# New priorities for the list schedule of a hybrid encoder's first phase, with both embedding projections ahead of its last scan

## The chip, the cores and the metric

The kernel runs on one core of one Trainium2 chip. The metric is device time in microseconds (us) of one execution, median over the runs shown. TensorE is called PE below, VectorE DVE, ScalarE ACT, GpSimd POOL, and SyncE SP; SP only issues transfers (DMA).

## The reference, cut to what matters

Two encoder layers over 512 tokens of width 1024, everything in fp32, with a ConvFFN of inner width 2816 and a gated embedding in each layer:

```python
def reference(x, p, ...):
    h = x
    for i in range(2):
        if i == 0:
            z = rmsnorm(h, mix_norm[0]) @ mix_w_in[0]
            y_a = rwkv7_bidir(z[..., :RWKV_COLS], ...)      # 8 heads x 64, one scan in each direction
            y_b = hyena_bidir(z[..., RWKV_COLS:], ...)      # 512 channels, long filters by FFT
            h = h + jnp.concatenate([y_a, y_b], axis=-1) @ mix_w_out[0]
        else:
            z = rmsnorm(h, na_norm[0]) @ na_w_qkv[0]
            h = h + neighbourhood_attention(z, ...) @ na_w_out[0]
        h = h + conv_ffn(h, ffn_norm[i], ffn_w_up[i], ffn_conv_w[i], ffn_conv_b[i], ffn_w_down[i])
        h = h + per_layer_embedding(h, p[i], ple_norm[i], ple_w_gate[i], ple_w_proj[i])
    return h

def per_layer_embedding(h, p_i, norm_g, w_gate, w_proj):
    return jax.nn.sigmoid(rmsnorm(h, norm_g) @ w_gate) * (p_i @ w_proj)
```

The product `p_i @ w_proj` (512x256 by 256x1024) depends on nothing else, so that it can be made at any time before its layer's end.

## The kernel before, in words

Tokens lie along the free axis, channels along the 128 partitions; a tile is 128x512. A product of fp32 operands is made as three matmuls (`mm3`): both operands are split into a high and a low part, ACT makes the high part by a cast and POOL the low part by a subtraction, and high x high, high x low and low x high are summed in PSUM.

Layer 0's mixing is the first phase (`mixer0`, `both_mixers`). The rest (`ffn`, `ple`, `mixer1`, and the same again) follows it, with `gemm` as its main loop; weights come there by `load_split` into `wraw` (128x1024), ACT casts them to `whi` (line L633), DVE makes `wlo` (L625), and PE multiplies them into the bank `g` (L619). In front of a `gemm` stands `norm`: for each of the eight tiles of h, ACT makes the scaled and split input `xh` and the square `nsq` (both L628; two buffers of `nsq`), and POOL adds the squares up one after the other (`nacc`, L625).

The first phase isn't written in the order of execution. An object `Plan` stands in for the compiler's engines: each call becomes one or more steps in a named group, 2741 steps in all; a step knows its engine, the steps it must come after, and a price (`Plan.note`, `price`). `ranks` gives each step the longest path of prices from it to the end, lifts it to at least the rank of its group's first step less `DRAG`, and adds 1000 times the priority of its group, from the tables `ORDER` and `MOVED` (method `order` of `Kern`). A list scheduler (`schedule`) then goes through the engines, takes the ready step of highest rank, and keeps account of free tiles, and `write` issues the steps in that order. `in_order` holds the compiler to it, each engine by itself. Since all steps are issued in `write`, every instruction of this phase has line L582 in the profile, and its names tell what it is.

The groups that matter here:

- `z`, `prep`, `inverse`, `scan`, `out`, each for m = 0 to 3: RWKV for two heads each. `z` is the input projection, `prep` (m, d) prepares direction d, and stores for `inverse` the products of 64x64 blocks that have to be inverted. `inverse` m loads those (tiles `nd`), solves on DVE by a row of small multiplications and reductions that grow from 128x1 to 128x225, stores the solution (`xd`), loads it back transposed (`w<-xd`, eight transfers), and goes on with matmuls `b<-w` 64x64 on PE. `scan` m then runs over eight chunks of 64 tokens, one after the other in a chain: matmuls of 64 columns into a bank (`b<-uv,w`, `b<-uv,dg`, `b<-x,uv`, `b<-r,w`), a copy from PSUM by ACT and DVE into `uv`, matmuls on that copy (`b<-x,uv`), and so on. Between two links of that chain PE can only do what other groups have ready.
- `hyena`, `filters`, `fparts`, `kf`, `signals`, `ab`, `back`: the long convolutions, as matmuls with tables of the Fourier transform (`dft_f`, `dft_i`). `kf` are the four transforms of the filters and `ab` those of the signals, 24 matmuls of 128x512 and less each, `back` the inverse transforms.
- `early`, `mid`, `last`: the output projection (`mix_w_out`) over parts of the channels. The last parts need the end of the last `scan` and of `back`.
- `emb` l: the projection `p @ w_proj` of layer l, 48 matmuls of 128x512. Its weights and inputs come through `wr` (`in_proj`, `in_pT`), its eight results go to DRAM (`pj_d_125` to `pj_d_132` for layer 0, `pj_d_133` to `pj_d_140` for layer 1), and `ple` loads them much later.

Loads of weights and tables go through three buffers `wr` and are issued by SP, which issues all transfers of the phase in one order and waits at the first that can't start. The parts made from them lie in twelve buffers `wp`; other tiles are `w`, of 39.

## Time and profile before

| | |
|---|---|
| median of three runs | 1597.96 us (1595.04 to 1604.57) |
| the profiled execution | 1599.19 us, of which 1597.4 us from the first to the last instruction |
| mean granted clock of PE | 0.976 |
| PE busy | 1527.6 us (96%) |
| DVE, ACT, POOL busy | 975.3 (61%), 718.5 (45%), 341.6 us (21%) |
| last matmul of the first phase | ends at 499.4 us |
| first matmul of the rest | starts at 508.25 us |

The page of a profile gives busy time by engine, then the span in 40 slices, the DMA queues, the chain of work that ended last, the costliest groups of instructions and the DMA issues. Answers of the trace used below are: the table of stretches (start:end, length, then busy us and count of instructions of PE, PE's weight loads, DVE, ACT and POOL, the granted clock of PE as a share of full speed, the busy share of the DMA engines, GB/s); the timeline of one engine (start, length, engine, line, instruction, count, and in brackets the idle time before it with what ended it); and groups by line and shape (count, busy us, mean ns of one, idle time before). A tile's name is shown without its number.

### The profile page before, as it was taken

The numbers are of one execution on the slowest core, as the hardware profiler recorded it, in microseconds if no ns is written. First come the engines' busy times: TensorE is split into PE (matmuls) and PEld (weight loads), VectorE is DVE, ScalarE is ACT, GpSimd is POOL, SyncE is SP. The second block draws the span as 40 slices with busy tenths as digits, with TensorE's granted clock in tenths as the row PEclk, the third lists the DMA queues.
The fourth block names the chain that finished last, engine by engine and source line by source line (L and its number), as shares of the span: only waits on it lengthen the run. The fifth ranks groups of instructions, "written<-read, shape, count | busy, mean of one in ns | idle before, by whom it ended". The sixth has DMA issues, their size and how long they took to land.

```text
span 1597.4 us, 24570 instructions
## 1 busy us (share of the span) xinstructions
PE 1527.6 (96%) x9520; PEld 1217.7 (76%) x9520; DVE 975.3 (61%) x1618; ACT 718.5 (45%) x1210; POOL 341.6 (21%) x296
## 2 busy tenths in 40 slices
PE   7999999979897999999999999999999999999997
PEld 6766777757585888888888878777778888888886
DVE  5875777865644567535675664555666664276654
ACT  5636464644444444313444554555554442244432
POOL 5664464443463000000002231021030000000020
PEclk9998999979898999999999999999999999999999
DMA  7456474777354223222342324223122332322421
GB/s 240 121 133 195 129 213 119 229 204 231 113 183 138 93 92 101 97 93 92 106 145 93 104 98 134 82 93 120 60 72 77 103 106 98 100 92 86 166 93 66
DMA packets 114583, 195.97 MB, mean 123 GB/s; under 512 B 27537, under 2 KB 57105, under 8 KB 114466
## 3 DMA queue, kind: packets, MB, share of 16 engines
q1 hardware_dynamic: 114466, 194.40, 38.5%
q8 instruction: 75, 1.23, 0.3%
q14 instruction: 42, 0.34, 0.1%
HBM read 163.95 MB, written 28.84 MB: 121 GB/s over the span
## 4 chain that ended last, share of the span: by engine, by line
PE 82%; DVE 6%; DMA 4%; ACT 3%; SPq 2%; issue 1%; POOL 1%; POOLq 0%; DVEq 0%; ACTq 0%
PE g L619 61%; PE b L582 17%; DVE w L582 4%; SPq L582 2%; PE m L619 2%; PE s L619 1%; DMA wr<-in_mix_w_in 1%; PE m L1878 1%; POOL w L582 1%; ACT w L582 1%; DMA w<-nd 1%; DMA wr<-in_dft_f 1%; POOL nacc L625 0%; ACT oh L633 0%; DVE uv L582 0%
## 5 line engine op out<-in xcount | busy, mean ns | idle before, releaser
L625 DVE TENSOR_TENSOR wlo<-wraw,whi 128x1024 fp32r<-128x1024 f32 x180 | 227.8, 1267 | 322.5 <-ACT whi L633 317.7
L633 ACT CAST whi<-wraw 128x1024 fp32r<-128x1024 f32 x180 | 188.2, 1046 | 406.7 <-PE g L619 398.5
L619 PE MATMUL g<-xh,whi 128*128 128x512 f32 x832 | 326.8, 393 | 8.9 <-ACT whi L633 8.9
L619 PE MATMUL g<-xh,wlo 128*128 128x512 f32 x832 | 325.3, 391 | 1.0 <-DVE wlo L625 1.0
L619 PE MATMUL g<-xl,whi 128*128 128x512 f32 x832 | 325.0, 391 | 0.0
L619 PEld LDWEIGHTS g<-xh,whi 128*128 128x128 f32 x832 | 157.0, 189 | 43.1 <-ACT whi L633 9.3
L619 PEld LDWEIGHTS g<-xh,wlo 128*128 128x128 f32 x832 | 156.8, 189 | 34.7 <-DVE wlo L625 1.7
L619 PEld LDWEIGHTS g<-xl,whi 128*128 128x128 f32 x832 | 157.1, 189 | 32.4
L625 POOL TENSOR_TENSOR nacc<-nsq 128x512 f32<-128x512 f32 x5 | 8.8, 1769 | 760.3 <-PE g L619 639.7
L582 PE MATMUL b<-xh,wp 128*128 128x512 f32 x432 | 149.9, 420 | 10.3 <-ACT wp L582 10.0
L619 PE MATMUL g<-hh,whi 128*128 128x512 f32 x352 | 137.2, 390 | 0.0
L619 PE MATMUL g<-hh,wlo 128*128 128x512 f32 x352 | 137.0, 389 | 0.0
L619 PE MATMUL g<-hl,whi 128*128 128x512 f32 x352 | 136.9, 389 | 0.0
L622 DVE SCALAR_TENSOR_TENSOR c<-u,prm,c 128x511 f32<-128x511 f32 x176 | 126.3, 746 | 6.4 <-ACT c L628 5.9
L582 PEld LDWEIGHTS b<-xh,wp 128*128 128x128 f32 x432 | 82.3, 195 | 35.1 <-ACT wp L582 12.0
L628 ACT ACTIVATE c<-u,prm 128x512 f32<-128x512 f32 x88 | 70.3, 817 | 70.8 <-DVE u L625 70.8
L582 POOL TENSOR_TENSOR wp<-wr,wp 128x512 fp32r<-128x512 f32 x62 | 83.1, 1352 | 48.2 <-ACT wp L582 41.3
L582 POOL TENSOR_TENSOR w<-w 128x256 f32<-128x256 f32 (+2 forms) x69 | 76.1, 1121 | 69.2 <-ACT w L582 51.8
L582 PE MATMUL b<-xl,wp 128*128 128x512 f32 x216 | 88.6, 416 | 0.0
L625 DVE TENSOR_TENSOR u<-g,rstd 128x512 f32<-128x512 f32 x104 | 71.3, 686 | 16.4 <-PE g L619 15.6
L582 DVE TENSOR_TENSOR w<-w 128x512 f32<-128x512 f32 (+16 forms) x116 | 69.1, 613 | 17.6 <-DMA w<-nd 10.7
L619 PE MATMUL g<-wlo,xh 128*128 128x512 f32 x192 | 77.2, 402 | 0.0
(181 smaller groups left out, 2608.1 us busy)
## 6 DMA issues: line engine op xcount, KB each, us to landing
wraw<-in_up SPq DMA_DIRECT2D x88, 512.0 KB, 3.5
wraw<-in_down SPq DMA_DIRECT2D x44, 512.0 KB, 3.5
wr<-in_mix_w_in SPq DMA_DIRECT2D x52, 256.0 KB, 3.8
wraw<-in_na_w_qkv SPq DMA_DIRECT2D x24, 512.0 KB, 3.5
x<-ch_d SPq DMA_DIRECT2D x16, 640.0 KB, 5.7
ch_d<-w SPq DMA_DIRECT2D x64, 128.0 KB, 2.2
wraw<-in_gate SPq DMA_DIRECT2D x16, 512.0 KB, 3.4
tab<-in_rpb SPq DMA_DIRECT2D x8, 768.0 KB, 4.2
```

The source lines that it names most:

```text
L582: getattr(e, method)(*args, **kw)
L619: return self.nc.tensor.matmul(out, lhsT, rhs, start=start, stop=stop, skip_group_check=not group)
L622: return self.nc.vector.scalar_tensor_tensor(out=out, in0=in0, scalar=scalar, in1=in1, op0=op0, op1=op1)
L625: return (eng or self.nc.vector).tensor_tensor(out=out, in0=in0, in1=in1, op=op)
L628: return self.nc.scalar.activation(out=out, in_=in_, func=func, **kw)
L633: self.nc.scalar.copy(h, src)
L1878: nc.tensor.transpose(pst[:, i], sc[:, i // 2, (i % 2) * P:(i % 2 + 1) * P], ident)
```

## The change

The code of the steps is the same, and the same 2741 steps come out with the same things that each must come after. What changes is the priorities, and through them each engine's order in the first phase; the order of all instructions after it is the same in both kernels. The embeddings `emb` go from 25 to 10 in the table, `kf` from 67 to 48, `ab` from 58 to 44, `signals` from 70 to 62, `mid` from 72 to 60, and `MOVED` gives fourteen groups a priority of their own. `DRAG` goes from 0 to 20, so that the steps of a group may differ in rank by up to 20. The other lines add prices for shapes that don't occur in this phase, a switch that has its old value, and a way to chain groups that isn't used here; line numbers grow by 8 or 9, so that the phase's instructions have line L590 in the changed kernel and those of the rest L627, L633, L641 and L655.

```diff
-    DRAG, SMALL = 0.0, 3
+    DRAG, SMALL = 20.0, 3
...
+        if engine == "tensor" or dma:
+            before = self.final.get((self.behind.get(self.group), engine))
+            if before is not None:
+                s.after[before.n] = True
+            self.final[self.group, engine] = s
...
+                if rows > 64 and n > 64:
+                    t = max(n / 2000, 0.057)
...
-                 hyena=50, fparts=40, kf=67, signals=70, ab=58, back=46, early=30, emb=25, consts=86, mid=72,
-                 last=99)
+                 hyena=50, fparts=40, kf=48, signals=62, ab=44, back=46, early=30, emb=10, consts=76, mid=60,
+                 last=99, norm1=98, next=40)
...
-    MOVED = {("back", 0): 57.5, ("back", 2): 35.5, ("early", 0): 28.5, ("hyena", 2): 26.5, ("kf", 0, 1): 30.5,
-             ("mid", 1): 32.5, ("scan", 0): 86.5, ("early", 1): 36.5}
+    MOVED = {("ab", 0): 84.5, ("ab", 1): 38.5, ("back", 0): 57.5, ("early", 1): 36.5, ("hyena", 2): 26.5,
+             ("inverse", 2): 88.5, ("kf", 0, 1): 30.5, ("kf", 1, 1): 49.5, ("mid", 0): 61.5, ("mid", 1): 32.5,
+             ("out", 3): 60.5, ("prep", 1, 0): 84.5, ("hyena", 0): 59.5, ("hyena", 3): 68.5}
```

Three places show what that makes of the order. The first is PE's queue at the end of scan 2, where no other group stood between the links of the chain before (`b<-w` 64x128 are the last products of `prep`, `b<-con,w` transposes):

```order
L582 MATMUL b<-x,uv 64x64 x4
L582 MATMUL b<-r_637,w 64x64 x4
L582 MATMUL b<-w 64x128 x7
L582 MATMUL b<-uv,x 64x64 x4
L582 MATMUL b<-x,uv 64x64 x4
L582 MATMUL b<-w 64x128 x11
L582 MATMUL b<-uv,w 64x64 x4
L582 MATMUL b<-uv,dg 64x64 x4
L582 MATMUL b<-con,w 128x128 x8
```

In the changed kernel the same chain has matmuls of 128x512 of hyena 2 (`xh`, `xl` with `wp`) between the copy's two ends:

```order
L590 MATMUL b<-uv,x 64x64 x4
L590 MATMUL b<-x,uv 64x64 x4
L590 MATMUL b<-xh_187,wp 128x512
L590 MATMUL b<-xh_190,wp 128x512
L590 MATMUL b<-xl_191,wp 128x512
L590 MATMUL b<-xh_190,wp 128x512
L590 MATMUL b<-xl_191,wp 128x512
L590 MATMUL b<-xh_190,wp 128x512
L590 MATMUL b<-xh_169,wp 128x512
L590 MATMUL b<-xl_170,wp 128x512
L590 MATMUL b<-uv,w 64x64 x4
L590 MATMUL b<-uv,dg 64x64 x4
```

Between links of scan 2 that had nothing between them stand now eight matmuls and more. Counted over the whole queue, 84 matmuls of 128x512 of other groups stand inside scan 2 (48 before), and 128 (44 before) between the last product that inverse 3's store needs and inverse 3's first matmul, among 344 matmuls of all kinds there (252 before). From the like product to inverse 1's first matmul there are 236 (386 before), 76 of them of 128x512 (86 before); for inverse 2 332 (362 before), 72 of 128x512 (82 before); for inverse 0 230 (222 before), 134 of 128x512 (122 before).

The second place is PE's queue where the phase ends and `g` begins. Before, 38 and ten more matmuls of layer 1's embedding (`b<-w,wp`) stand there, among those of the output projection:

```order
L582 MATMUL b<-w,wp 128x512 x38
L582 MATMUL b<-xh_811,wp 128x512
L582 MATMUL b<-xl_812,wp 128x512
L582 MATMUL b<-xh_811,wp 128x512
L582 MATMUL b<-xl_812,wp 128x512
L582 MATMUL b<-xh_811,wp 128x512
L582 MATMUL b<-xl_812,wp 128x512
L582 MATMUL b<-xh_811,wp 128x512 x3
L582 MATMUL b<-w,wp 128x512 x2
L582 MATMUL b<-xh_811,wp 128x512
```

In the changed kernel the phase ends with the output projection alone:

```order
L590 MATMUL b<-xh_811,wp 128x512 x4
L590 MATMUL b<-xh_1143,w 128x512
L590 MATMUL b<-xh_1145,w 128x512
L590 MATMUL b<-xl_1146,w 128x512
L590 MATMUL b<-xh_1145,w 128x512
L590 MATMUL b<-xl_1146,w 128x512
L590 MATMUL b<-xh_1145,w 128x512
L590 MATMUL b<-xl_1146,w 128x512
L590 MATMUL b<-xh_1145,w 128x512
L627 MATMUL g<-xh_6042,whi 128x512
```

Behind the last matmul of scan 3 stand 160 matmuls of 128x512 (212 before) and 84 of 128x256 (96 before). Inside scan 3 there are 96 of other groups' 128x512 in both kernels.

The third place is SP's queue at the same boundary. Before, the stores of layer 1's embedding stand ahead of the first load of the next stage:

```order
L582 DMA wr<-in_mix_w_out_b 128x512 x8
L582 DMA wr<-in_proj 128x512 x3
L582 DMA wr<-in_mix_w_out_b 128x512
L582 DMA wr<-in_proj 128x512
L582 DMA wr<-in_mix_w_out_b 128x512
L582 DMA pj_d_133<-w 128x512
L582 DMA pj_d_134<-w 128x512
L582 DMA pj_d_135<-w 128x512
L582 DMA pj_d_136<-w 128x512
L582 DMA pj_d_137<-w 128x512
L582 DMA pj_d_138<-w 128x512
L582 DMA pj_d_139<-w 128x512
```

In the changed kernel the loads of `wraw` follow the last loads of `wr`:

```order
L590 DMA w<-bon_d_116 128x512
L590 DMA wr<-in_dft_i 128x512 x2
L590 DMA w<-in_xT 128x512
L590 DMA wr<-in_mix_w_out_a 128x512 x3
L590 DMA w<-in_xT 128x512 x3
L590 DMA wr<-in_mix_w_out_b 128x512 x10
L655 DMA wraw<-in_up 128x1024 x24
```

All sixteen stores of `pj_d` have moved ahead of the end of scan 3. One of them, `pj_d_125`, stands now between inverse 3's store of `xd` and its eight loads `w<-xd`; 19 loads into `wr` (eight of `in_proj`, four of `in_pT`, seven of `dft_f`) stand in SP's queue around that place.

9 lines of the change are left out of this document (5 added, 4 removed).

## The prediction

> **What bounds the kernel now.** I read the page's share of engines and its chain of waits first:
>
> ```profile
> PE 1527.6 (96%) x9520; PEld 1217.7 (76%) x9520; DVE 975.3 (61%) x1618; ACT 718.5 (45%) x1210; POOL 341.6 (21%) x296
> PE 82%; DVE 6%; DMA 4%; ACT 3%; SPq 2%; issue 1%; POOL 1%; POOLq 0%; DVEq 0%; ACTq 0%
> PE g L619 61%; PE b L582 17%; DVE w L582 4%; SPq L582 2%; PE m L619 2%; PE s L619 1%; DMA wr<-in_mix_w_in 1%; PE m L1878 1%; POOL w L582 1%; ACT w L582 1%; DMA w<-nd 1%; DMA wr<-in_dft_f 1%; POOL nacc L625 0%; ACT oh L633 0%; DVE uv L582 0%
> ```
>
> PE is busy for 96% of the span and makes 82% of the chain. Both kernels give PE the same matmuls, so only two things can change: the time in which PE waits, and the time in which its clock is at half speed. I call both together the loss. The second view, the table of stretches, shows where it is. The cuts are at places named below: 320.6 is the end of the last product that inverse 3's store needs (p), 360.7 inverse 3's first matmul (q), 378.4 to 433.4 is scan 3, 499.4 the phase's last matmul.
>
> ```profile
> 20.00:320.60 300.60, 287.75 (x3133) 216.34 (x3133) 218.02 (x422) 160.80 (x340) 161.96 (x158) 0.97 0.57 163
> 320.60:360.70 40.10, 29.30 (x255) 22.02 (x255) 27.40 (x66) 17.35 (x41) 17.31 (x16) 0.79 0.72 210
> 360.70:378.40 17.70, 17.33 (x301) 13.58 (x301) 8.63 (x16) 7.91 (x17) 5.66 (x5) 1.00 0.88 284
> 378.40:433.40 55.00, 46.86 (x467) 34.43 (x467) 35.13 (x55) 21.79 (x59) 25.00 (x21) 0.88 0.42 134
> 433.40:499.40 66.00, 63.75 (x320) 51.77 (x318) 31.95 (x48) 27.37 (x48) 29.39 (x24) 1.00 0.44 146
> 499.40:508.20 8.80, 0.00 (x0) 0.00 (x0) 2.52 (x4) 6.52 (x12) 3.97 (x4) 0.69 0.83 298
> 508.20:516.50 8.30, 7.28 (x16) 5.28 (x17) 5.50 (x3) 3.66 (x5) 7.52 (x4) 0.50 0.52 145
> 516.50:1597.00 1080.50, 1064.24 (x5001) 866.10 (x4999) 633.59 (x990) 459.70 (x670) 83.52 (x49) 0.99 0.30 99
> 339.00:356.00 17.00, 11.17 (x71) 8.81 (x72) 14.16 (x33) 6.38 (x15) 6.90 (x5) 0.50 0.74 246
> ```
>
> Per microsecond the loss is largest in four places: p to q (idle 10.8 of 40.1, clock 0.79), scan 3 (idle 8.1, clock 0.88), and the boundary in two rows (8.8 with nothing done, then 8.3 at clock 0.50). The tail after scan 3 loses 2.25 of 66, and all behind 516.5 is the same code in the same order. So the change is worth what it does to p to q, scan 3, the boundary and the long early stretch.
>
> The timeline of PE shows what the idle time from p to q is:
>
> ```profile
> 313.13 0.45 PE L582 MATMUL b<-uv,x 128*64 128x64 f32 x8 [1.62 <-DVE uv L582]
> 319.52 1.08 PE L582 MATMUL b<-w 64*64 64x128 f32 x22
> 337.01 0.45 PE L582 MATMUL b<-uv,w 128*64 128x64 f32 x8 [2.95 <-ACT uv L582]
> 337.39 0.45 PE L582 MATMUL b<-uv,dg 64*64 64x64 f32 x8
> 345.27 1.02 PE L582 MATMUL b<-x,uv 128*64 128x64 f32 x8 [2.56 <-ACT uv L582]
> 348.06 2.93 PE L582 MATMUL b<-w,wp 128*128 128x512 f32 x6 [1.77 <-ACT wp L582]
> 360.67 1.55 PE L582 MATMUL b<-w 64*64 64x64 f32 x42
> ```
>
> PE waits for scan 2's own copies (`uv`) with nothing else to do, while the solve of inverse 3 goes on elsewhere; from 339 on the clock is at half speed too.
>
> **The change, part by part.** *Work and loss from p to q.* At full speed the work is 29.30 less half of the 11.17 done at half speed, 23.7; the loss is 40.1 - 23.7 = 16.4 us. The price of what is moved in comes from groups by line and shape, the first row from 484 to 499.4, the second from 435 to 484:
>
> ```profile
> L582 PE MATMUL b<-w,wp 128*128 128x512 f32 x48 | 11.6, 394 | 0.0
> L582 PE MATMUL b<-w 128*128 128x256 f32 x96 | 12.7, 288 | 0.6 <-POOL w L582 0.6
> ```
>
> The first gives 11.6/48 = 0.242 us each, the second 0.132. There are 128 matmuls of 128x512 from p to q instead of 44: 84 x 0.242 = 20.3 us. Small ones come at 0.38 per eight (337.01 to 337.39), 0.047 each, and the eight other matmuls that are more add 0.4. The work is 44.4 us. The chain behind p (store, loads, DVE's solve, store, loads) took 40.1 in the trace, itself stretched by what else DVE and SP did, so it is covered by work alone with some 4 us over. Where are the 84 from? 36 are hyena 2's, which stood ahead of p, the others are the embeddings' and filter transforms'. No work vanishes, so I count losses only. What loss stays: the last chunk of scan 2 is still bare by the order; I leave it 3 us of waits (2.56 was one before) and 1.5 for a half-speed stretch of 3.4 us. The term is 16.4 - 4.5 = **11.9 us gained**. The bounds: nothing gained, if what is moved in isn't ready (rival 2), and 16.4.
>
> *Scan 2 ahead of p.* The last ten microseconds:
>
> ```profile
> 311.00:321.00 10.00, 7.53 (x150) 6.55 (x148) 9.65 (x19) 4.97 (x14) 4.38 (x4) 0.83 0.42 141
> ```
>
> The idle time is 2.5, and clock 0.83 is 3.4 us at half speed, worth about 1.3. The order puts hyena 2's matmuls into nine links that were bare (the fences on scan 2), eight at a time, 8 x 0.242 = 1.9 us against a wait of 1.62. Of 3.8 lost I take **3 as gained**. Half speed began here although no wait was longer than 1.62. The Trainium skill ("TensorE: Matmul & The Clock Gate", section "Why this matters for your kernels") asks for no idle gaps of PE above about 3 us to keep the clock; by that rule a bare chunk with waits like these would cost no clock at all, and the sum would come out 1.5 us lower. The trace shows otherwise, and I stay with the trace.
>
> *q to scan 3, and scan 3.* The first lost 0.4 and is full still. In scan 3 the order has 96 matmuls of 128x512 of others as before, and as many bare links but one; its loss of 8.1 idle plus the half-speed stretches stays: **0**. It could lose or gain 3 us by where the cover falls.
>
> *The tail.* 52 x 0.242 + 12 x 0.132 = 14.2 us of work leave it, but that is work made elsewhere. The cover that it gave is gone: the last split of a weight was early enough before,
>
> ```profile
> L582 POOL TENSOR_TENSOR wp<-wr,wp x62: 1266/1293/1845, 7.2 to 481.7; 128x512 fp32r<-128x512 f32 x62
> ```
>
> at 481.7 + 1.3 = 483.0, 49.6 us behind scan 3's end, with six pieces of the embedding loaded and split among them. Without these (6 x 1.29 = 7.7 us of POOL) some 42 us; the work left is 66 - 2.25 - 14.2 = 49.6. So the splits end ahead of PE by 7 us: **0**, at most 5 lost.
>
> *The boundary.* ACT, PE and SP there:
>
> ```profile
> 498.30 2.03 ACT L582 COPY w<-b 128x512 f32<-128x512 f32 x4
> 500.20 1.97 ACT L628 ACTIVATE xh<-h,prm 128x512 fp32r<-128x512 f32 x3
> 504.63 1.15 ACT L628 ACTIVATE nsq<-h 128x512 f32<-128x512 f32 x2 [1.43 <-POOL nacc L625]
> 506.63 0.63 ACT L628 ACTIVATE nsq<-h 128x512 f32<-128x512 f32 x1 [0.85 <-POOL nacc L625]
> 507.17 1.03 ACT L633 CAST whi<-wraw 128x1024 fp32r<-128x1024 f32 x1
> 508.25 0.79 PE L619 MATMUL g<-xh,whi 128*128 128x512 f32 x1 [8.87 <-ACT whi L633]
> 493.77 6.93 SPq L582 DMA_DIRECT2D pj_d<-w  x8
> 500.80 25.77 SPq L647 DMA_DIRECT2D wraw<-in_up  x8
> ```
>
> The first `g` waited for the cast `whi`, and two queues held that: SP issued the first `wraw` at 500.80, behind eight stores of the embedding; and ACT came to the cast at 507.17 only, behind four copies of the embedding, `xh`, and squares that waited for POOL's sums (1.43 and 0.85). The change frees SP of the stores and ACT of the copies (2.0 us). The squares still stand ahead of `whi` in ACT's queue. From the last addition to h: 0.7 for it, 0.65 for an `xh`, a square 0.6, one wait near 0.9, a square 0.6, the cast 1.0: about 4.5 us instead of 8.9, **4.4 gained**. The half-speed stretch (7.28 busy at 0.50, a loss of 3.6) gets perhaps 0.6 shorter, together **5**. Bounds: 0, if the sums on POOL set it as before, and 8.8.
>
> *SP.* The store `pj_d_125` now stands ahead of the eight `w<-xd` of inverse 3; it waits for an embedding's matmuls and ACT's copy, and behind it wait those loads and then q. The cover of p to q exceeds the chain by 44.4 + 4.5 - 40.1 = 8.8 us, and a delay below that costs nothing: **0**.
>
> *The early part, 20 to p.* The loss is 12.9 us of idle time, and clock 0.97 is 18 us at half speed, some 9 us: 22, of which 3.8 are counted above. The order shifts nearly everything here. Covers of the inverses' chains, as stretches from the like of p to the like of q for m = 0, 1, 2:
>
> ```profile
> 76.30:118.30 42.00, 38.26 (x222) 28.53 (x223) 32.85 (x73) 15.62 (x25) 25.75 (x27) 0.96 0.51 130
> 168.70:210.80 42.10, 38.77 (x389) 29.00 (x388) 27.84 (x68) 16.11 (x39) 19.31 (x20) 0.96 0.41 106
> 241.80:279.00 37.20, 36.00 (x366) 26.16 (x365) 28.44 (x66) 18.02 (x42) 17.49 (x18) 1.00 0.44 110
> 210.76 1.15 PE L582 MATMUL b<-w 64*64 64x64 f32 x32 [0.89 <-POOL w L582]
> ```
>
> By the counts of the order, m = 0 gets 12 more of 128x512 (+2.9), m = 1 loses 10 of them and 140 small ones (2.4 + 6.6 = 9.0, leaving 29.8), m = 2 loses 10 and 20 (3.4, leaving 32.6). Against that, PE itself waited only 0.89 for inverse 1's chain, so the 42.1 is what PE's queue made of it, not its floor; the floor isn't in the trace. I take **1 lost**, between 15 gained (most of the remaining 18) and the 28 of rival 1.
>
> The sum: -11.9 - 3 - 5 + 1 = -18.9 against the profiled execution's 1599.19: 1580.3. That execution was 1.2 above the median, so against the median 1579; I say **1580**.
>
> **Rivals.** *1, slower: the chains of inverse 1 and 2 come bare.* If they take 42.1 and 37.2 as before, the cover is short by 12.3 and 4.6, against 3.3 and 1.2 lost before: 12.4 us more, and each bare stretch may draw a half-speed one like that of 339 to 356, 17 us, worth up to 8.5. With both, 28.4 more: some **1608**. It decides from 26 us of loss in the early part. For it: the shorter cover is certain; against it: the 0.89 above, and the solve competes with less other work. Chance 0.09.
>
> *2, about the same: the hole is one of buffers.* The matmuls moved into it need 19 loads through three buffers `wr`, and PE's wait at 348.06 was for such a part, not for the scan. SP's row:
>
> ```profile
> 341.20 5.61 SPq L582 DMA_DIRECT2D wr<-in_proj  x2
> ```
>
> That is 2.8 us a load, 53 us for 19, and from p to scan 3 there are 44.4 + 4.5 + 17.7 = 66.6. From 3.5 us a load on, the embedding comes too late and PE waits as before; scan 2 and the boundary still gain: 1599 - 8 = **1591** or a little more. Chance 0.15. The Trainium skill ("Perfetto Trace Analysis", section "Optimization Strategy") reads a repeated gap on the engine that should be saturated as a possible sign of too few buffers; by it the changed order would leave the gap. The waits of 2.95 and 2.56 for `uv` say that most of this gap isn't that.
>
> *3, more: the early part gains as well*, 10 of its 18 us: **1570**. Chance 0.13. *4: the tail misses its cover* by 5 to 8 us: 1587. Chance 0.04.
>
> **Chances and range.** The forecast (1572 to 1588) has 0.59. About 0.5%, 8 us, is what a measurement of this kernel can tell from no change, so faster means below 1590 and slower above 1606. Faster: 0.59 + 0.13 + 0.01 of the tail's case = 0.73. Same: rival 2 and the rest of 4, 0.18. Slower: 0.09. The range 1566 to 1597 takes in most of rivals 2 and 3 and leaves out rival 1 and the far end of rival 3.
>
> **What would show it.** From p to q the clock is above 0.9 and the idle time below 5; scan 3 starts near 377 (378.4 less the 13.9 gained ahead of it, plus 12.8 us of work that stands ahead of it now: 14.2 from the tail less 1.4 that went inside scan 3) and takes 55 to 57 us; the phase's last matmul ends near 485; the first `wraw` is issued before that, and `g` starts some 4.5 us behind it. It is wrong if idle time of more than 5 us stands ahead of inverse 1 or 2, if PE waits for `wp` in front of the embedding's matmuls, or if the first `g` still starts 8 us behind.

## The result, and the profile after

The changed kernel takes 1611.51 us (median of 16 runs, 1603.98 to 1625.72), the kernel before 1601.95 beside it (16 runs, 1593.82 to 1606.17). The ratio is 1.0078 with an interval of 1.0061 to 1.0094: slower by about 0.8%, where 1580 and faster was predicted. The profiled execution took 1610.59 us, of which 1608.8 are the span, 11.4 more than the one before.

The page of the changed kernel, busy shares and the chain of waits:

```profile
PE 1536.1 (95%) x9520; PEld 1221.2 (76%) x9520; DVE 976.2 (61%) x1618; ACT 717.9 (45%) x1208; POOL 342.6 (21%) x296
PE 85%; DMA 4%; DVE 3%; ACT 3%; SPq 2%; issue 1%; POOL 1%; DVEq 0%; ACTq 0%; POOLq 0%
```

The line of engine shares in the second row reads DVE 6% in the kernel before and here 3%: DVE left the chain and PE took its place, which alone would look like an improvement. But PE's busy time rose from 1527.6 to 1536.1 us with the same 9520 matmuls, so more of them ran at half speed. The table of stretches of the changed kernel, cut at the places that answer to those of the prediction (326.2 is p, 386.0 q, 406.4 to 460.1 scan 3, 513.1 the phase's last matmul, 518.2 the first `g`):

```profile
20.00:326.20 306.20, 284.85 (x3083) 210.43 (x3081) 209.30 (x412) 153.10 (x325) 159.15 (x155) 0.94 0.55 155
326.20:386.00 59.80, 50.29 (x344) 37.41 (x344) 41.22 (x80) 27.43 (x58) 29.42 (x24) 0.86 0.63 197
386.00:406.40 20.40, 18.83 (x310) 14.71 (x309) 7.76 (x15) 12.37 (x29) 6.25 (x6) 1.00 1.02 305
406.40:460.10 53.70, 47.03 (x478) 35.30 (x477) 33.88 (x55) 23.93 (x60) 25.65 (x22) 0.90 0.47 156
460.10:513.10 53.00, 51.42 (x258) 42.86 (x256) 24.41 (x38) 19.32 (x33) 19.94 (x16) 0.97 0.45 155
513.10:518.20 5.10, 0.00 (x0) 0.00 (x0) 4.76 (x8) 4.09 (x8) 4.14 (x3) 0.98 0.00 0
285.70:326.20 40.50, 39.71 (x707) 30.43 (x702) 29.45 (x59) 22.61 (x57) 18.49 (x18) 1.00 0.72 209
```

Read against the rows in the prediction: from p to q the idle time is 9.5 us (10.8 before) at clock 0.86, where below 5 and above 0.9 were predicted, so the hole is still there. The last row is the stretch from inverse 2's first matmul to p: 0.8 idle at full speed. The tail is 53.0 long instead of 66, and 5.1 us pass before the first `g` instead of 8.8. And the first row, from which some 2 us were to be gained, went from clock 0.97 to 0.94 and from 12.9 to 21.4 us idle. Its cuts, of the changed kernel:

```profile
0.00:118.80 118.80, 99.14 (x582) 73.69 (x582) 78.38 (x142) 58.84 (x96) 68.88 (x79) 0.93 0.58 169
209.30:285.70 76.40, 71.08 (x903) 53.14 (x904) 56.69 (x113) 37.54 (x86) 41.23 (x41) 0.96 0.59 161
```

and the like places of the kernel before:

```profile
0.00:118.30 118.30, 104.83 (x634) 79.55 (x635) 82.86 (x151) 61.65 (x101) 69.51 (x84) 0.99 0.56 163
210.80:279.00 68.20, 66.55 (x838) 49.57 (x839) 53.66 (x110) 39.90 (x88) 37.87 (x36) 1.00 0.63 175
279.00:320.60 41.60, 38.56 (x700) 30.19 (x702) 35.55 (x62) 27.14 (x69) 18.33 (x17) 0.96 0.72 220
```

Inverse 0's first matmul starts at the same time in both (118.8, 118.3), but with 52 matmuls fewer done and a clock of 0.93 instead of 0.99. A ledger puts that in microseconds. The loss up to a place is its time less the work that PE has done by then, each matmul at the full-speed duration of its like in the profile of before. The last column is what the prediction gave for the same stretch:

| up to | loss before | loss after | change in this stretch | predicted |
|---|---|---|---|---|
| inverse 0's first matmul | 12.5 | 26.1 | +13.6 | |
| inverse 2's first matmul | 29.5 | 49.5 | +6.4, with the row above +20.0 | +1 |
| q | 56.4 | 69.9 | -6.5 | -14.9 |
| the phase's last matmul | 71.7 | 85.4 | +0.2 | 0 |
| the first `g` | 80.5 | 90.5 | -3.7 | -4.4 |
| the end | | | +1.4 | -0.6 |
| sum | | | +11.4 | -18.9 |

So 19 of the 30 us of error lie in the early part and 8 around the hole. In single traces such a ledger scatters: two of the kernels below have the same order up to scan 3 (*Its loads first* and *And the link first*), and yet inverse 1's first matmul comes at 204.4 in one and at 210.7 in the other. So a difference of less than some 6 us between two traces, summed up to a place, shows nothing by itself, and verdicts on time go by several runs.

The timeline of the changed kernel at the hole, PE first, then ACT, DVE and SP:

```profile
345.02 3.78 PE L590 MATMUL b<-w,wp 128*128 128x512 f32 x8 [5.70 <-ACT wp L590]
363.32 11.29 PE L590 MATMUL b<-w,wp 128*128 128x512 f32 x38
386.01 2.08 PE L590 MATMUL b<-w 64*64 64x64 f32 x64
344.35 0.62 ACT L590 CAST wp<-wr 128x512 fp32r<-128x512 f32 x1 [6.64 <-DMA wr<-in_dft_f]
346.57 0.69 DVE L590 TENSOR_TENSOR w<-w 128x512 f32<-128x512 f32 x1 [1.92 <-DMA w<-hw_d]
338.81 0.91 SPq L590 DMA_DIRECT2D wr<-in_dft_f  x2
```

PE's longest wait is 5.70 us in front of matmuls of a filter's transform: their part `wp` waits for ACT's cast, the cast waited 6.64 for a load, and SP issued that load at 338.81 only, behind a row of stores and of `w<-hw_d` (the windowed filters). The same wait stands in the three other traces with this order of loads (*Spread*, *And supply*, *And chain* below), with 6.07, 5.79 and 5.07. The 128 large matmuls were there as counted, but the ones that stood first in PE's queue weren't ready, and scan 2's next link stood behind them; 38 others ran in one piece at 363.32, when scan 2 was over. At q PE itself didn't wait: its queue set q, not the inverse.

The timeline of the changed kernel in the early part:

```profile
61.34 0.50 PE L590 MATMUL b<-xh,wp 128*128 128x512 f32 x1 [2.57 <-ACT wp L590]
76.05 1.12 PE L590 MATMUL b<-con,w 128*128 128x128 f32 x4 [2.12 <-POOL w L590]
75.96 4.27 POOL L590 TENSOR_TENSOR wp<-wr,wp 128x512 fp32r<-128x512 f32 x3
57.58 0.54 SPq L590 DMA_DIRECT2D wr<-in_mix_w_in  x1
81.29 0.54 SPq L590 DMA_DIRECT2D wr<-in_mix_w_in  x1
```

and the stretch inside it in which the clock is at half speed:

```profile
67.40:81.10 13.70, 9.78 (x27) 5.87 (x26) 11.88 (x17) 2.71 (x5) 12.83 (x12) 0.50 0.63 155
```

No wait is above 2.57 us, but from 67.4 to 81.1 PE has 27 matmuls only, 18 of `prep` and from 77.45 on nine of `z`, and runs at half speed, while DVE (11.88 of 13.7) and POOL (12.83) are full. SP issued no load of an input weight from 57.58 to 81.29; POOL's three splits at 75.96 come behind `prep`'s additions. How many of the `z` matmuls (those with `wp`) fall between 60 and 80 shows the difference, before:

```profile
60.00:80.00 20.00, 13.68 (x54) 9.46 (x54) 1.85 (x3) 6.46 (x5) 1.00 0.59 168
```

and after:

```profile
60.00:80.00 20.00, 3.28 (x8) 2.37 (x9) 0.62 (x1) 4.04 (x3) 0.69 0.58 152
```

54 before and 8 after (busy us and count of PE, its weight loads, ACT and POOL). These are the two things that the runs had to explain: the loss that is new in the early part, and the hole that stayed.

### The profile page after: what moved, and what is told of

Same layout as the page of the kernel before. It is cut to its first block, busy times and chain, and to the rows that moved or that the text cites. A ratio compares the mean times of both kernels' runs of the same rounds, so it can differ in the third digit from the quotient of the medians.

```text
span 1608.8 us, 24543 instructions
## 1 busy us (share of the span) xinstructions
PE 1536.1 (95%) x9520; PEld 1221.2 (76%) x9520; DVE 976.2 (61%) x1618; ACT 717.9 (45%) x1208; POOL 342.6 (21%) x296
## 4 chain that ended last, share of the span: by engine, by line
PE 85%; DMA 4%; DVE 3%; ACT 3%; SPq 2%; issue 1%; POOL 1%; DVEq 0%; ACTq 0%; POOLq 0%
PE g L627 61%; PE b L590 20%; DMA wr<-in_mix_w_in 2%; SPq L590 2%; DVE w L590 2%; PE m L627 1%; PE s L627 1%; ACT w L590 1%; DMA w<-kt_d 1%; PE m L1887 1%; POOL nacc L633 0%; ACT oh L641 0%; ACT wp L590 0%; DVE ol L633 0%; DVE uv L590 0%
## 5 line engine op out<-in xcount | busy, mean ns | idle before, releaser
L633 DVE TENSOR_TENSOR wlo<-wraw,whi 128x1024 fp32r<-128x1024 f32 x180 | 228.0, 1269 | 315.3 <-ACT whi L641 306.4
L641 ACT CAST whi<-wraw 128x1024 fp32r<-128x1024 f32 x180 | 188.2, 1046 | 408.3 <-PE g L627 400.2
L627 PE MATMUL g<-xh,whi 128*128 128x512 f32 x832 | 326.9, 393 | 5.1 <-ACT whi L641 5.1
L627 PE MATMUL g<-xh,wlo 128*128 128x512 f32 x832 | 325.0, 391 | 2.3 <-DVE wlo L633 2.3
L627 PE MATMUL g<-xl,whi 128*128 128x512 f32 x832 | 325.1, 391 | 0.0
L627 PEld LDWEIGHTS g<-xh,whi 128*128 128x128 f32 x832 | 157.0, 189 | 39.3 <-ACT whi L641 5.5
L627 PEld LDWEIGHTS g<-xh,wlo 128*128 128x128 f32 x832 | 157.0, 189 | 36.1 <-DVE wlo L633 3.0
L627 PEld LDWEIGHTS g<-xl,whi 128*128 128x128 f32 x832 | 157.1, 189 | 32.2
L633 POOL TENSOR_TENSOR nacc<-nsq 128x512 f32<-128x512 f32 x5 | 8.8, 1768 | 753.3 <-PE g L627 639.6
L590 PE MATMUL b<-xh,wp 128*128 128x512 f32 x432 | 153.4, 424 | 13.8 <-ACT wp L590 13.3
L627 PE MATMUL g<-hh,whi 128*128 128x512 f32 x352 | 137.2, 390 | 0.0
L627 PE MATMUL g<-hl,whi 128*128 128x512 f32 x352 | 137.0, 389 | 0.0
L627 PE MATMUL g<-hh,wlo 128*128 128x512 f32 x352 | 136.9, 389 | 0.0
L590 PEld LDWEIGHTS b<-xh,wp 128*128 128x128 f32 x432 | 82.8, 197 | 37.3 <-ACT wp L590 15.3
L590 POOL TENSOR_TENSOR wp<-wr,wp 128x512 fp32r<-128x512 f32 x62 | 82.4, 1342 | 91.0 <-ACT wp L590 46.0
L590 PE MATMUL b<-xl,wp 128*128 128x512 f32 x216 | 90.7, 420 | 0.2 <-issue 0.2
L590 POOL TENSOR_TENSOR w<-w 128x256 f32<-128x256 f32 (+2 forms) x69 | 77.4, 1140 | 58.0 <-ACT w L590 46.5
L633 DVE TENSOR_TENSOR u<-g,rstd 128x512 f32<-128x512 f32 x104 | 71.3, 686 | 16.4 <-PE g L627 15.5
L627 PE MATMUL g<-whi,xh 128*128 128x512 f32 x192 | 77.2, 402 | 0.0
L627 PE MATMUL g<-wlo,xh 128*128 128x512 f32 x192 | 77.2, 402 | 0.0
```

What stands on the lines that cost most here:

```text
L590: getattr(e, method)(*args, **kw)
L627: return self.nc.tensor.matmul(out, lhsT, rhs, start=start, stop=stop, skip_group_check=not group)
L633: return (eng or self.nc.vector).tensor_tensor(out=out, in0=in0, in1=in1, op=op)
L641: self.nc.scalar.copy(h, src)
```

## The experiments

Each ratio is to runs of the kernel before on the same chip, with its 95% interval. All of these kernels have the same steps; only their order differs.

**Where the early loss comes from.** The first set takes the change apart. *The new tables with the old DRAG*:

```diff
-    DRAG, SMALL = 20.0, 3
+    DRAG, SMALL = 0.0, 3
```

> The changed kernel's tables ORDER and MOVED, with DRAG back at 0. By the order, the first p comes then behind about as much of PE's work as in the kernel before (69 us against 67.8; 53 with the change), the hole from p to q of m = 3 has 37 us of cover and both embeddings are done ahead of scan 3's end. Theory A (DRAG makes the early loss: it draws the small steps of prep 0 together, with no matmul of 128x512 among them from 62 to 77 us): the loss up to inverse 0's first matmul falls from 19.6 us of idle and 17.5 us of half speed to about the 13.4 and 3.4 of the kernel before, the time is 1611.5 - 13 = 1598 or less. Rival B (the priority of prep 1, 0 makes it): the early loss stays, 1608 to 1614.

1595.25 us (1590.08 to 1599.02), ratio 0.9968 (0.9953 to 0.9984): a little faster than before. Its row of `wp` matmuls from 60 to 80, and its hole:

```profile
60.00:80.00 20.00, 13.07 (x52) 9.01 (x50) 1.86 (x3) 6.27 (x5) 1.00 0.56 162
311.30:369.40 58.10, 44.40 (x443) 33.11 (x440) 38.91 (x80) 28.61 (x68) 27.32 (x23) 0.85 0.72 221
```

With 52 of them PE keeps full speed as before; the loss up to q is 55.8 against 56.4 before and 69.9 after. The same shows up to inverse 2's first matmul, in idle time of PE and time at half clock: 28.4 and 34.1 us in the changed kernel, 30.9 to 35.5 and 34.1 to 37.5 in the four runs below that keep its tables and DRAG (*Spread*, *And supply*, *And chain*, *Loads first*), here 23.3 and 10.2, and 18.7 and 17.1 in the kernel before. So the early loss belongs to DRAG, and the hole (13.7 idle, clock 0.85) does not.

*DRAG alone*, in the kernel before:

```diff
-    DRAG, SMALL = 0.0, 3
+    DRAG, SMALL = 20.0, 3
```

> The kernel before with DRAG at 20 and its own tables. The first p comes behind 52.6 us of PE's work; layer 1's embedding stays in the tail; the hole of m = 3 has 14 us of cover (21.6 before) and scan 2 only 8 matmuls of 128x512 inside. Theory A (DRAG makes the early loss): some 13 us more up to inverse 0's first matmul and 5 to 10 more from scan 2 to inverse 3, 1615 to 1625. Rival B (the tables' priority of prep 1, 0 makes the early loss): the early part as before, 1605 to 1612.

1654.49 us, ratio 1.0339 (1.0314 to 1.0364). That is far more than the early part. Its tail:

```profile
447.90:553.00 105.10, 81.52 (x362) 63.13 (x362) 42.55 (x55) 36.70 (x64) 45.44 (x35) 0.89 0.38 126
```

With the old tables, DRAG puts the matmuls of both embeddings (96 `b<-w,wp`, 48 before) behind scan 3, where 23.6 us are idle, and 10.9 more pass before `g`. *The change without its entry for prep 1, 0* does the same to a lesser degree:

```diff
-             ("out", 3): 60.5, ("prep", 1, 0): 84.5, ("hyena", 0): 59.5, ("hyena", 3): 68.5}
+             ("out", 3): 60.5, ("hyena", 0): 59.5, ("hyena", 3): 68.5}
```

> The changed kernel without the priority of its own for prep 1, 0, DRAG 20 as in the change. The first p comes behind 52.6 us of PE's work (53.0 with the change) and layer 1's embedding returns to the tail. Theory A (DRAG makes the early loss): up to inverse 0's first matmul idle time and half speed stay as in the changed kernel (19.6 and 17.5 us), the time is 1608 or more. Rival B (prep 1, 0 ahead of the matmuls of 128x512 makes it): the stretch from 62 to 77 us holds 128x512 matmuls again, 10 to 13 us less there.

1639.87 us, ratio 1.0243 (1.0216 to 1.0271): the tail is 85 us with 9.2 idle, since layer 1's embedding is back in it, and most of the loss up to inverse 1 stays (35.7 against 38.8 in the changed kernel and 25.9 before). That entry isn't what costs most of the early time; with DRAG it is what holds the embedding ahead of scan 3's end.

*DRAG for prep 0 only*, in the changed kernel:

```diff
-            s.rank = max(s.rank, self.firsts[s.group].rank - self.DRAG)
+            s.rank = max(s.rank, self.firsts[s.group].rank - (self.DRAG if s.group[:2] == ("prep", 0) else 0.0))
```

> The changed kernel with DRAG for the groups prep 0 alone. The first p comes behind 61.5 us of PE's work (69.0 with the new tables and no DRAG, 53.0 with the change), the hole from p to q has 40 us of cover. Theory A (DRAG's loss comes from prep 0, whose small steps it draws ahead of the matmuls that covered them): the loss up to inverse 1's first matmul grows by 5 to 8 us against the tables without DRAG, 1600 to 1604. Rival B (it comes from other groups, z and the filters): 1593 to 1597 as with the tables without DRAG.

1608.47 us (1607.36 to 1617.55), ratio 1.0069 (1.0047 to 1.0091). The step from 0.9968 to 1.0069 is DRAG in one pair of groups, and the changed kernel's 1.0078 lies inside the interval. Its `wp` matmuls from 60 to 80, its first 121.7 us, and the stretch from inverse 2's first matmul to p:

```profile
60.00:80.00 20.00, 9.82 (x38) 6.52 (x37) 1.24 (x2) 2.64 (x2) 0.96 0.55 152
0.00:121.70 121.70, 102.69 (x608) 76.04 (x609) 79.92 (x148) 59.75 (x99) 68.96 (x80) 0.94 0.57 169
292.80:328.90 36.10, 31.97 (x501) 24.67 (x500) 25.38 (x46) 18.89 (x44) 11.18 (x11) 0.81 0.76 230
```

The thinning is less than with DRAG everywhere, but 19.0 us are idle and the clock is 0.94 up to inverse 0, where the kernel before has 13.5 and 0.99. Yet the same time as the changed kernel's doesn't mean the same loss in the same place. Up to inverse 2's first matmul this kernel is idle for 22.7 us and at half clock for 23.9, the tables without DRAG for 23.3 and 10.2, the changed kernel for 28.4 and 34.1. In its trace most of what this run loses to the tables alone comes later: from inverse 2's first matmul to p, 4.1 us are idle at clock 0.81, with the tables alone 0.5 at full speed. That DRAG makes the early loss is shown by these runs, and that DRAG in prep 0, on top of the tables, costs 1.0 points of ratio; that the changed kernel's early loss comes from prep 0 is not, and the agreement of the two times is in part chance. How DRAG acts is the next question.

**How the early loss comes about.** DRAG lets the steps of prep 0 that lie on the longest path overtake the others and the next `z`. The first theory was that PE's order is at fault: `z` matmuls are bunched behind 77 us instead of standing between the small steps. *Spread*: 22 of them are put back between the steps of `prep` in PE's queue, with two of POOL's splits moved ahead:

```diff
+            by = {s.n: s for s in order}
+            moves = {560: (531, 540), 592: (533, 534), 598: (535, 536), 227: (537, 541), 225: (542, 543), 612: (544,),
+                     233: (545, 546)}
+            gone = {n for v in moves.values() for n in v}
+            order = [t for s in order if s.n not in gone for t in (s, *(by[n] for n in moves.get(s.n, ())))]
```

> The changed kernel, with 22 matmuls of 128x512 of z 1 (5.3 us) taken forward in PE's queue and spread among the small steps of prep 0 and prep 1, 0, where from 62 to 77 us none stood; the two splits on POOL that they need go ahead of prep 0's operations there (2.9 us earlier work on POOL). Everything else keeps its order. Theory A (the early loss is made by the small steps drawn together without cover, 5.1 us of waits and 13.7 us at half speed from 67.4): the waits from 62 to 78 fall from 6.9 to below 3.5, the half-speed stretch to 7 or less, the first inverse's first matmul comes 5 to 8 us earlier than 118.8, the time is 1611.5 - 6 = about 1605. Rival B (POOL and DVE set the pace there, so that the small steps only come later): less than 2 us of change at inverse 0's first matmul, 1609 to 1613.

*And supply*: two loads of weights and their casts and splits are moved forward too:

```diff
-                     233: (545, 546)}
+                     233: (545, 546), 320: (578, 972), 603: (571,), 605: (579, 973), 609: (580,)}
```

> The run with 22 matmuls spread, and besides: two loads of weights into wr (the last of z 1 and one of z 2) stand on SP ahead of prep 0, 0's stores, at about 61 us instead of 81, and the casts on ACT and splits on POOL of three weights (two of z 1, one cast of z 2) go forward with them. Theory C (the early part lacks weights, not cover in PE's queue: by 80 us the changed kernel had issued 15 loads into wr and made 14 splits, the kernel before 21 and 19, since a wr buffer is held until POOL's split and the splits and loads stand behind the steps of prep 0 that DRAG drew ahead): PE's waits for wp (0.75, 3.55 and 0.30 us from 78 to 88) fall below 1 in sum, the first inverse's first matmul comes 4 to 6 us earlier than 120.3, the time is about 1606. Rival D (POOL as a whole sets the pace, what goes forward there only delays prep): less than 2 us at inverse 0's first matmul, 1610 to 1614.

*And chain*: besides, an addition of `z` 1 on DVE and four steps of prep 1, 0 come earlier:

```diff
-                     233: (545, 546), 320: (578, 972), 603: (571,), 605: (579, 973), 609: (580,)}
+                     233: (545, 546, 547, 606), 320: (578, 972), 603: (571,), 605: (579, 973), 609: (580,), 1805: (607,), 974: (615, 621)}
```

> The run with the early supply of weights, and besides the chain of prep 1, 0 taken forward: PE waited 8.25 us at 84.8 for a product of it on POOL, which waited for a scaling on ACT (at 90.2), which waited for z 1's addition on DVE (at 88.4), which stood behind the start of inverse 0's solve, itself waiting for its loads until 86.0. That addition goes ahead of the solve, and the four steps that follow from it on ACT, DVE and POOL go ahead of z 2's cast and split. Theory E (the early loss is queueing: steps ready by 76 us stand on the in-order engines behind steps that wait for late loads): the wait of 8.25 falls below 2, the first inverse's first matmul comes at 114 to 117 instead of 122.3, the time is 1604 to 1607. Rival D (the work of POOL and DVE as a whole sets the pace of the early part): less than 2 us at inverse 0's first matmul, 1610 to 1614.

1612.45 us, ratio 1.0073 (1.0050 to 1.0095); 1613.08, 1.0082 (1.0060 to 1.0104); 1609.99, 1.0062 (1.0039 to 1.0086). None of the three can be told from the changed kernel's 1.0078. The stretch 60 to 80 of the first did what it was to do:

```profile
60.00:80.00 20.00, 17.36 (x132) 12.23 (x132) 14.99 (x27) 8.69 (x14) 13.80 (x16) 0.93 0.54 147
```

(over all of PE's matmuls; 13.80 busy at 0.69 in the changed kernel). But in its timeline a wait of 3.55 for the next weight's part appears behind it:

```profile
86.61 0.63 PE L590 MATMUL b<-xh,wp 128*128 128x512 f32 x1 [3.55 <-ACT wp L590]
```

With the supply moved that wait is gone, and the timeline has one of 8.25 in its place:

```profile
93.08 3.94 PE L590 MATMUL b<-w 64*64 64x128 f32 x64 [8.25 <-POOL w L590]
```

With the chain moved that is down to 0.5, and another link waits:

```profile
91.93 2.08 PE L590 MATMUL b<-w,con 128*128 128x512 f32 x2 [5.03 <-DVE w L590]
```

Inverse 0's first matmul comes at 120.3, 122.3 and 120.3, against 118.8. So moving these `z` matmuls in PE's queue doesn't mend it, nor does removing any one of these waits: taking one away uncovers the next, on ACT, POOL, then DVE. The reading that fits all three is that the queues of POOL, DVE and SP in that part, which DRAG has ordered anew as well, set the pace together. That is argued from the row of 67.4 to 81.1 and from these waits; which of the three engines' orders would have to be put back is left open.

**Why the hole stayed.** *Loads first*: in the changed kernel three of the late loads of `dft_f` go ahead of the sixteen `w<-hw_d` in SP's queue:

```diff
+            early = [s for s in order if s.engine == "sync" and s.group in (("kf", 0, 0), ("kf", 1, 0))][:3]
+            order = [s for s in order if s not in early]
+            at = next(i for i, s in enumerate(order) if s.engine == "sync" and s.group == ("fparts", 0))
+            order[at:at] = early
```

> The changed kernel, with the order of all engines kept but for three loads: the first three loads of the filter transforms' tables (wr<-in_dft_f) stand on SP ahead of the sixteen loads w<-hw_d instead of behind them, some 20 us earlier. Theory A (the hole from p to q is now one of late table loads: SP reaches them only at 338.8, PE waits 5.70 us for the part made from them with scan 2's next link queued behind it, and the clock goes to half speed from 343.9 to 354.1): the wait of 5.70 falls below 1, the half-speed stretch goes or gets shorter, p to q goes from 59.8 to about 51, the time from 1611.5 to about 1603. Rival B (the twelve buffers wp, or inverse 3's solve, hold PE at the same place): p to q stays within 2 us of 59.8 and the time within 3 us of the changed kernel.

1609.65 us (1605.11 to 1614.61), ratio 1.0053 (1.0031 to 1.0076). The hole of that kernel in the table of stretches:

```profile
337.00:391.60 54.60, 45.22 (x346) 33.96 (x344) 40.33 (x79) 27.67 (x58) 29.54 (x24) 0.97 0.65 198
```

and in its timeline the longest wait, and one of the additions that DVE had ahead of the copy:

```profile
357.99 0.69 PE L590 MATMUL b<-uv,x 128*64 128x64 f32 x8 [5.17 <-DVE uv L590]
350.86 0.69 DVE L590 TENSOR_TENSOR w<-w 128x512 f32<-128x512 f32 x1 [2.17 <-DMA w<-hw_d]
```

The wait of 5.70 for `wp` is gone, and p to q is 5.2 us shorter with the clock at 0.97. The idle time is 9.4 as before: a wait of 5.17 for scan 2's copy took its place, since DVE has the copy in its queue behind additions that wait for `w<-hw_d`. That the late load makes the first wait is shown; that it makes the hole is not. The time isn't clear of the changed kernel's, and the 5.2 us may be scatter: *And chain*, in which these loads are as late as ever, has nearly the same row with the wait in it.

```profile
331.20:386.80 55.60, 45.33 (x346) 33.86 (x344) 40.77 (x79) 27.62 (x58) 29.42 (x24) 0.97 0.68 210
349.43 3.61 PE L590 MATMUL b<-w,wp 128*128 128x512 f32 x8 [5.07 <-ACT wp L590]
```

*The embedding moved alone*: the kernel before with one entry more in `MOVED`:

```diff
-    MOVED = {("back", 0): 57.5,
+    MOVED = {("emb", 1): 55, ("back", 0): 57.5,
```

> The kernel before with one priority more: layer 1's embedding at 55. PE's order is the one before up to the middle of scan 2; from there the embedding stands in scan 2's end, the hole from p to q and scan 3 (80 matmuls of 128x512 of others inside scan 2 instead of 48, 25.8 us of work from p to q instead of 21.6, 188 behind scan 3 instead of 212), and its stores come ahead of the tail. Theory A (the terms of the prediction hold where the early part is left alone): 3 us less in scan 2, 4 in the hole, 4 to 5 at the boundary: about 1589 against 1600. Rival B (the hole is held by late loads with the scan's steps queued behind them, so that matmuls moved there don't fill it): the loss from p to q stays at 16 us or grows, only the boundary gains: 1595 to 1598.

1601.25 us (1592.38 to 1605.40), ratio 0.9999 (0.9980 to 1.0018): no change.

```profile
321.50:362.70 41.20, 32.20 (x270) 23.52 (x270) 30.41 (x62) 20.03 (x48) 21.48 (x17) 0.83 0.66 206
500.20:505.50 5.30, 0.04 (x1) 0.04 (x1) 5.30 (x9) 5.14 (x8) 0.95 (x1) 0.76 0.00 0
```

The boundary is 5.3 us, as with the whole change, so that part is the embedding's stores and copies leaving the tail. The hole is idle for 9.0. Moving the embedding "into the middle" is worth nothing by itself that the time shows, the shorter boundary included.

*hyena 3 alone*: again one entry, which brings both embeddings ahead of scan 3's end as well:

```diff
-    MOVED = {("back", 0): 57.5,
+    MOVED = {("hyena", 3): 68.5, ("back", 0): 57.5,
```

> The kernel before with one entry of the new table: hyena 3 at 68.5. It moves that block's matmuls ahead, keeps the first p behind 67.8 us of PE's work as before, and so brings both embeddings into the middle (98 matmuls of 128x512 of others inside scan 2, 39.1 us of work from p to q, 164 of 128x512 behind scan 3). Theory A (cover is what the hole lacked): 3 + 11.9 + 5 less, about 1580. Rival B (late loads hold the hole whatever stands in it): some 13 us of idle time and 17 at half speed from p to q as with the new tables without DRAG, 1592 to 1597.

1589.14 us (1585.74 to 1601.86), ratio 0.9940 (0.9919 to 0.9961): this one entry of the change, without the rest, gains 0.6%. Its hole:

```profile
313.50:369.20 55.70, 45.25 (x406) 34.10 (x404) 39.97 (x82) 28.18 (x65) 26.11 (x22) 0.85 0.71 217
```

and in its timeline the longest wait there, the addition and the copy on DVE, and SP:

```profile
325.47 0.69 PE L582 MATMUL b<-uv,x 128*64 128x64 f32 x8 [4.26 <-DVE uv L582]
324.39 0.69 DVE L582 TENSOR_TENSOR w<-w 128x512 f32<-128x512 f32 x1 [3.00 <-DMA w<-hw_d]
325.12 0.29 DVE L582 TENSOR_SCALAR uv<-b 64x128 f32<-64x128 f32 x1
316.31 5.00 SPq L582 DMA_DIRECT2D ch_d<-w  x7
321.36 3.46 SPq L582 DMA_DIRECT2D w<-hw_d  x7
```

PE waits 4.26 for scan 2's copy at 325.12; DVE could make it only behind an addition that waited 3.00 for a load of `hw_d`; SP issued that load at 321.36, behind seven stores. *Its loads first*: the eight `w<-hw_d` and three `wr<-in_dft_f` are put ahead of eleven stores in SP's queue (numbers are those of steps):

```diff
+            early = [s for s in order if s.engine == "sync" and (s.group == ("fparts", 1) or s.group in (("kf", 0, 0), ("kf", 1, 0)) and s.n in (2184, 2185, 2197))]
+            order = [s for s in order if s not in early]
+            at = next(i for i, s in enumerate(order) if s.n == 1594)
+            order[at:at] = early
```

> The kernel before with hyena 3 at 68.5, and in its order eleven loads moved ahead on SP: the eight of the second half of the filters' parts (w<-hw_d) and three of the transforms' tables (wr<-in_dft_f) stand ahead of eleven stores of prep 3, 1 and inverse 3 that wait for ACT and DVE, some 8 us earlier; PE, DVE, ACT and POOL keep their order. Theory A (the hole is made by late loads: DVE's copy for scan 2's next link stands behind an addition that waits for w<-hw_d, landed at 324.3, and PE waits 4.26 us for that copy): the wait of 4.26 falls below 1.5, the half-speed stretch of 17.1 us from 319.5 falls to 7 or less, p to q from 55.7 to about 48, the time from 1589 to about 1581. Rival B (SP's issue or the DMA engines are full there, so that what is moved ahead delays the stores by as much): p to q stays within 2 us, the time within 3 us of 1589.

1586.31 us (1585.78 to 1588.71), ratio 0.9912 (0.9886 to 0.9938). Its timeline and, below, its hole:

```profile
315.39 4.29 SPq L582 DMA_DIRECT2D w<-hw_d  x8
325.53 0.45 PE L582 MATMUL b<-uv,x 128*64 128x64 f32 x8 [2.54 <-DVE uv L582]
```

```profile
315.50:369.60 54.10, 45.17 (x408) 33.74 (x404) 41.13 (x82) 28.10 (x65) 27.16 (x22) 0.91 0.73 224
```

The loads come 6 us sooner, the wait falls from 4.26 to 2.54 (2.26 in the next run, which has the same order there), and the hole's clock rises from 0.85 to 0.91 (0.87 in the next run). So the late loads make part of that wait. They aren't shown to make the hole: p to q is 1.6 us shorter, 8.9 us stay idle, and the time's interval overlaps that of hyena 3 alone (0.9919 to 0.9961). By its numbers the rival of that expectation, no more than 2 us in the hole and 3 in the time, is what came. *And the link first*: two operations of `ab` 1 on DVE go behind a copy of scan 3.

```diff
+            late = [s for s in order if s.n in (2354, 2357)]
+            order = [s for s in order if s not in late]
+            at = next(i for i, s in enumerate(order) if s.n == 1755) + 1
+            order[at:at] = late
```

> The kernel of the run with the eleven loads moved, and on DVE two of ab 1's operations (1.78 and 0.68 us) behind the copy for scan 3's next link instead of ahead of it. Theory (the same queueing in scan 3: PE waited 2.73 us at 423.7 for a copy that stood behind other groups' work on DVE): the wait falls below 0.8, the half-speed stretch of 6.8 us from 425.3 goes, some 4 us less than the run without this edit. Rival: the copies wait for PE's own chain, no difference above 1 us.

1586.72 us (1579.48 to 1595.48), ratio 0.9912 (0.9882 to 0.9942). The trace shows the effect, a wait of 2.66 in scan 3 that is now 0.76, and scan 3 in 45.6 us instead of 48.7:

```profile
394.30:439.90 45.60, 41.03 (x461) 29.87 (x460) 30.67 (x50) 22.36 (x58) 23.95 (x19) 0.99 0.50 160
```

The time doesn't show it: what one copy's delay is worth is below what these runs can tell. Both versions are faster than either kernel of the case, by 0.9% against the kernel before.

## Why the prediction was wrong, and where it was right

*Right: the boundary and the tail.* The first `g` was to start some 4.5 us behind the phase instead of 8.9. The timeline of the changed kernel there:

```profile
495.58 27.36 SPq L655 DMA_DIRECT2D wraw<-in_up  x4
517.14 1.03 ACT L641 CAST whi<-wraw 128x1024 fp32r<-128x1024 f32 x1
518.23 0.80 PE L627 MATMUL g<-xh,whi 128*128 128x512 f32 x1 [5.12 <-ACT whi L641]
```

5.12, with `wraw` issued 17.5 us ahead of the phase's end and the squares ahead of the cast as the prediction had them. Every kernel whose embeddings left the tail has 5.1 to 5.3 here, the one with the embedding alone included. The tail took 53.0 us; the prediction's 66 less 14.2 is 51.8. The 1.2 more isn't idle time (1.6 us against 2.25 before), but comes with a stretch at half clock (0.97).

*Scan 2 ahead of p, as predicted in the trace but not firm; scan 3 right.* From inverse 2's first matmul to p 3.0 us were idle before, at clock 0.96, and 0.8 at full speed after; 3 us of gain was predicted. But the four other traces with that order of matmuls need 40.9 to 45.9 us there, against 40.5 in this one and 41.6 before, and three of them have half-speed time in it, so that the gain there is within the scatter. Scan 3 took 53.7 us, 55.0 before; below the 55 to 57 said.

*Wrong: the early part, +1 predicted and +20 measured up to inverse 2's first matmul.* The step that failed is the count of cover. It looked at how many matmuls stand between p and q for m = 0, 1, 2 and found inverse 1 and 2 short of cover, and inverse 0 with 2.9 us more. The loss came at inverse 0, and none of it as a wait in front of an inverse: p came at 67.3 instead of 76.3, q came no sooner (118.8 against 118.3), though the count gave this stretch 2.9 us more work as cover, so that the stretch grew from 42.0 to 51.5 us. What the count leaves out is the time ahead of p and the helpers: that p is early means that something else has been put off, here the `z` matmuls and the loads and splits that feed them (8 against 54 of them in 20 us). The clause to suspect was DRAG, the one part of the change that reorders all groups at once; the prediction gave it no price of its own. By itself it costs 3.4%, and in prep 0, on top of the new tables, 1.0 points of ratio; the new tables without it lose nothing against before up to q (55.8 against 56.4). Through which of the groups it makes the early loss, and on which engine, stays open.

*Wrong: the hole, -11.9 predicted.* The stretch from inverse 2's first matmul to q gained 6.5, of which scan 2 ahead of p is about 4 by its idle time and clock, so that 2 to 3 are left for the hole. By the prediction's own count it is less: 59.8 us less the 44.4 of work is 15.4, against 16.4 before. The work moved in was sized well (all 128 matmuls ran there). The step that failed is "what loss stays": 4.5 us were left for bare links because covered ones were taken as lossless. In the trace the cover waited 5.70 for its own load, and cover that waits is no cover; in a queue served in order it also holds up the link behind it. That is the way of rival 2 (the hole is one of loads), with 0.15, though not by its arithmetic: it priced the rate of loads into `wr`, 2.8 us each, where it was the place of a few loads in SP's queue, `hw_d` among them, which don't go through `wr`. The wait for a copy (`uv`) that the profile names was read as the scan's own latency; in two of the runs the copy was late because DVE waited for a load first. When loads were put ahead, 9.4 and 8.9 us of the hole stayed idle, so what else holds it open isn't known.

*The rivals.* The time came out near rival 1's 1608, but by luck and not by its mechanism: no wait of more than 0.1 us stands in front of inverse 1's or 2's first matmul, and from inverse 0's to inverse 1's the loss grew by 12.7 us (25.9 - 12.5 = 13.4 before). The test that it set, more than 5 us idle ahead of inverse 1 or 2, isn't met (3.3 and 4.6 us in all between p and q there); the second, PE waiting for `wp` in front of the embedding's and transforms' matmuls, is (5.70). The range's upper end, 1597, was drawn from the hole's bounds; the 28 us that the early part was allowed to lose were kept out of it by a chance of 0.09 for the one mechanism thought of.

*What the change is worth, in parts.* Boundary: 3.7 us in the trace, of 4.4 predicted; the run with the embedding alone has it too and its time doesn't show it. The tables without DRAG: ratio 0.9968. DRAG in prep 0 on top of them: about +0.010. And of the tables, one entry (hyena 3) is worth 0.6% alone, by the medians more than all of them together, though the two intervals touch.

## What to carry to other kernels

When a list schedule is given new priorities, price the clause that touches every group first, and read the order on the helper engines and on the queue of loads where the first long chain begins, not only the matmul count at the known hole. Work moved into a gap covers it only if its inputs are there (here 5.07 to 6.07 us of wait in four traces): follow the first piece moved in back to the load that feeds it, and see what stands ahead of that load. A wait that names an engine's copy may be that engine's wait for a transfer one instruction earlier in its queue. Then measure whether taking the wait away gains time: here another took its place.

## What the runs showed of the hardware

Every stretch of half clock in these traces lasts 3.4 us or a multiple (3.4, 6.8, 10.2, 13.7, 17.1, 20.5), but for the last one of each, of 5.2 to 8.4 us, with which the trace ends. The Trainium skill ("TensorE: Matmul & The Clock Gate", section "Part 1: The HAM clock gate") gives the clock a free-running window of 3413 ns, and the lengths agree with that. How long a stretch lasts doesn't follow from the longest wait: in the changed kernel a wait of 2.57 that ends at 61.3 us, then waits of up to 2.12 among small matmuls, go with 13.7 us at half speed, while in the run with the loads first the wait of 5.17 costs 3.4:

```profile
357.90:361.30 3.40, 3.31 (x14) 2.66 (x15) 3.26 (x6) 0.98 (x2) 3.40 (x4) 0.50 0.62 116
```

Nor does it follow from the order alone: behind the wait for the late load the changed kernel, *Spread*, *And supply* and *And chain*, all with one order there, ran at half clock for 10.2, 10.2, 6.8 and 3.4 us.

What the traces show instead is how busy PE is from window to window. I cut the first 515 us of all fourteen traces (from 20 us on) into windows of 3.413 us, on whose edges the stretches begin. Of 70 windows at full speed in which PE was busy for less than 45%, 69 are followed by one at half speed; of 1499 with more than 80%, 13 are, and all of these hold matmuls of one or two columns (`b<-con,w` 128x1 and 128x2), so that busy time alone isn't all of it; of the 200 between, 47. Of 79 windows at half speed with PE busy for less than 80%, none is followed by full speed; of 168 above that, 127 are. Half speed began at 315.1 us in the kernel before, behind a window with 1.26 us of work in which no wait was longer than 1.62. So the rule that the Trainium skill gives on the same page, section "Why this matters for your kernels", no idle gaps above about 3 us, isn't enough here: waits of 2.57 and less went with a loss of the clock.
